# The start of the first FFN: two contraction tiles multiplied before their shift is known

## The chip, the cores and the metric

The kernel runs on one core of one Trainium2 chip. The metric is device time in microseconds (us) of one execution. Five engines work side by side, each on its own list of instructions: TensorE (PE, with its weight loads shown apart as PEld), VectorE (DVE), ScalarE (ACT), GpSimd (POOL) and SyncE (SP), which here issues most transfers. They meet through semaphores.

## The reference, cut to what matters

One layer of a diffusion backbone over 256 latent tokens and 256 context tokens of width 2048. The change touches only the entry of the first half-step FFN:

```
def adaln(x, g, mod, i):
    return rms_norm(x, g) * (1 + mod[:, i + 1, None, :]) + mod[:, i, None, :]

def half_step_ffn(x, mod, i, g, w_up, w_down):
    h = adaln(x, g, mod, i)
    a, b = jnp.split(h @ w_up, 2, axis=-1)
    return x + 0.5 * mod[:, i + 2, None, :] * ((jax.nn.silu(a) * b) @ w_down)
```

`mod` is `silu(c) @ w_mod + b_mod`, with one condition `c` for the latents and one for the context; `i` is 0 here. So the input of the product `h @ w_up` needs two modulation vectors of 2048 numbers for each of the two sequences: the scale `mod[1]` and the shift `mod[0]`. Each is a product of the condition with a 2048 x 2048 slice of `w_mod`, 16 MB to load. The mixer, the second FFN and the final norm follow and are not touched.

## The kernel before

The contraction of 2048 is cut into 16 tiles of 128 rows, k = 0 to 15. All matrix products keep fp32 accuracy by splitting each operand into a rounded high part and a low remainder: `hhi` and `hlo` hold the modulated and transposed tokens, one 512-wide column block per tile (256 context tokens, then 256 latents), and a product is three matmuls, high by high, low weights by high, high weights by low tokens.

The first stage, up to line 700, prepares the modulated tokens tile by tile and at once multiplies them with the first six column blocks of `w_up` (`NPRE = 3` pairs), which collect in six PSUM banks `pre`. It goes through `BLOCKS` (line 47): tile 0 alone, tile 1 alone, then pairs of tiles. For each block it needs the scale and the shift of those tiles and the weights.

- `mod_unit` (line 558) loads 1 MB of modulation weights from `w_m0` into one of four buffers `mraw`, in the order in which `_laid_out` (line 2388) wrote them.
- `mod_sums(i, k0, k1)` (line 565) multiplies such units with the two conditions on TensorE into a bank from `tbank`, of which there are two, and copies the result to a `row` on ScalarE. `i` is 0 for the shift and 1 for the scale.
- `mod_turned` (line 591) transposes the rows on TensorE, and VectorE adds up their four parts and the bias, into `SH` (shift) and `SC` (scale). `scale_of` (line 218) adds one and multiplies by the norm's gain.
- For a pair of tiles, the shift of the first one comes by another way: its weights lie still as rows, and VectorE multiplies them with the spread condition `cB` and sums (line 669). The shift of the second comes by `mod_sums`.
- `x_turned` and `to_hT` transpose the tokens of a tile on TensorE into a bank from `tbank`; `affine_split` (line 382) turns that bank into `hhi` and `hlo`: ScalarE and VectorE both apply scale and shift, and VectorE takes the difference.
- `products` (line 409) is a generator: its first step loads the weights of a block, its second splits them, and each of six further ones multiplies one unit: three matmuls for a block of one tile, six for a pair.

In the loop over `BLOCKS[1:]` (line 657) the products of one block are spread between the sums and transposes of the next one: `steps(prods, n)` puts n units at that place. `AHEAD` says how many units stand before and behind the groups of sums in the first rounds; later it is none before and one behind each group, one behind the row transposes, and what is left (`drain(prods)`) behind the transposes of the tokens. TensorE and VectorE are pinned to the order of the program in this stage, ScalarE until the block of tiles 2 and 3, and SP's loads are pinned too. `idle` issues products with no use, as fillers for waits (`N_IDLE`).

Buffers are taken in turn: whoever takes a third `tbank` waits until all readers of the first one are done, and a load into a fifth `mraw` waits on SP until one of the four before it has been read.

The first tile, in lines 637 to 656, has the shift's unit first, then the scale's, then the weights. When the stage ends, the next column blocks of `w_up` follow on all 16 tiles (`mm3`, line 150), which read the same `hhi` and `hlo`.

Of the kernel before, what the change touches and what calls it, by code (L numbers as in the profile page):

```python
# [19 lines left out]
P = 128  # L20
# [15 lines left out]
AHEAD = {1: (2, 2, 1), 2: (2, 2, 1, 1)}  # L36
# [24 lines left out]
def tile_layer(ctx: ExitStack, tc: tile.TileContext, I: dict, out: bass.AP):  # L61
# [405 lines left out]
    with pool(name="st", bufs=1) as st:  # L467
# [3 lines left out]
        stack = st.tile([32, P], F32, name="stack")  # L471
        pin(nc.vector.tensor_copy(stack[:, :96].rearrange("p (j q) -> p j q", j=3), ident[:32, :32].unsqueeze(1).to_broadcast([32, 3, 32])))
        sel = st.tile([96, P], BF16, name="sel")[:, :32]
# [14 lines left out]
        thirds = st.tile([96, P], BF16, name="thirds")  # L488
        middle = st.tile([96, P], BF16, name="middle")
        over = st.tile([96, P], F32, name="over")  # L490
# [4 lines left out]
        vector[0].tensor_tensor(thirds[64:96], over[64:96], middle[64:96], op=ALU.subtract)  # L495

# [53 lines left out]
        def x_scaled(k, tb):  # L550
            w = lambda x: x[:, k, :].rearrange("p (s c) -> p s c", s=2)
            affine_split(tb.rearrange("p (s c) -> p s c", s=2), 0, ((k, CTX), (k, LAT)), w(hhi), w(hlo))

# [11 lines left out]
        def mod_sums(i, k0, k1, last=iter(())):  # L565
# [17 lines left out]
            row = st.tile([P, 256], F32, tag="row", name="row", bufs=3)[:, :n]  # L583
# [64 lines left out]
        h0 = st.tile([P, 2, 256], F32, tag="h", name="h", bufs=2)  # L648
        hs = [slice(s * 256, (s + 1) * 256) for s in (CTX, LAT)]
        cols = [(SC[:, 0, s, 0:1], SH[:, 0, s, 0:1]) for s in (CTX, LAT)]  # L650
        for s in (CTX, LAT):
            scalar[0].activation(hhi[:, 0, hs[s]], first_tb[:, hs[s]], AF.Identity, scale=cols[s][0], bias=cols[s][1])
        scalar[0].activation(h0[:, CTX], first_tb[:, hs[CTX]], AF.Identity, scale=cols[CTX][0], bias=cols[CTX][1])
        vector[0].tensor_scalar(h0[:, LAT], first_tb[:, hs[LAT]], *cols[LAT], op0=ALU.mult, op1=ALU.add)
        vector[0].tensor_tensor(hlo[:, 0], h0.rearrange("p s c -> p (s c)"), hhi[:, 0].bitcast(F32), op=ALU.subtract)
        others(1, True)
        for k0, k1 in BLOCKS[1:]:
            kk = slice(k0, k1)
            following = products(1, pre, k0, k1, hhi, hlo, middle=True)
            if k1 - k0 == 2:  # L660
                raw = mod_unit()
            ahead = iter(AHEAD.get(k0, ()))
            steps(prods, next(ahead, 0))
            for i in range(2):
                for _ in mod_sums(i, k0 if i else k1 - 1, k1, following if i else iter(())):
                    steps(prods, next(ahead, 3 - (k1 - k0)))
                if not i and k1 - k0 == 2:
# [16 lines left out]
            if k1 - k0 == 1:  # L684
                tb = tbank()
                for s in (CTX, LAT):
                    for t in range(2):
                        x_turned(k0, s, t, tb)
                x_scaled(k0, tb)
            else:  # L690
                for s in (CTX, LAT):
                    drain(to_hT([xs0[s, 0], xs0[s, 1]], 0, s, hhi, hlo, 256 * s, range(k0, k1)))
# [1695 lines left out]
def _laid_out(a):  # L2388
# [23 lines left out]
    def block(k0, k1):  # L2412

        still = [wm[:, 0, k0 * P : (k0 + 1) * P].T[None]] if k1 - k0 == 2 else []
        return still + [units(0, k1 - 1, k1), units(1, k0, k1)]
# [53 lines left out]
```

## Time and profile before

| | |
|---|---|
| median of 3 runs | 2595.6 us (2595.38 to 2599.9) |
| profiled execution | 2594.48 us, span 2592.8 us |
| PE busy | 2566.9 us (99%) |
| DVE busy | 2183.1 us (84%) |
| ACT busy | 1432.8 us (55%) |
| the first stage | up to 133.14 us, when the first product at line 154 starts |
| rounds of a pair of tiles | 13.14 us each from 58.87 us on |

Line 89 in the profile is the helper that pins instructions, so the first stage's instructions show that line; they are told apart by the tiles they write and read: `tr<-mraw,cP` are the modulation sums, `tr<-ident,row` the row transposes, `tr<-ident,xs` the transposes of the tokens, `mm<-hhi,hi`, `mm<-hhi,lo` and `mm<-hlo,hi` the products. A row of the timeline gives the start, the length, the engine, the line, the operation and the count of what was merged; in brackets stands the idle time before it and what ended it. Matmuls overlap their successors, so the step from start to start is the cost of one, not its length.

### The profile page before, as it was taken

The numbers are of one execution on the slowest core, as the hardware profiler recorded it, in microseconds if no ns is written. First come the engines' busy times: TensorE is split into PE (matmuls) and PEld (weight loads), VectorE is DVE, ScalarE is ACT, GpSimd is POOL, SyncE is SP. The second block draws the span as 40 slices with busy tenths as digits, with TensorE's granted clock in tenths as the row PEclk, the third lists the DMA queues.
The fourth block names the chain that finished last, engine by engine and source line by source line (L and its number), as shares of the span: only waits on it lengthen the run. The fifth ranks groups of instructions, "written<-read, shape, count | busy, mean of one in ns | idle before, by whom it ended". The sixth has DMA issues, their size and how long they took to land. (4 is left out here: it accounts for less than half of the span.)

```text
span 2592.8 us, 34296 instructions
## 1 busy us (share of the span) xinstructions
PE 2566.9 (99%) x12716; PEld 2141.8 (83%) x12716; DVE 2183.1 (84%) x2884; ACT 1432.8 (55%) x1838; POOL 221.3 (9%) x273
## 2 busy tenths in 40 slices
PE   8999999999999999999999999999999999999998
PEld 5788888888888888888889989888898888888886
DVE  6788888878888788888887889798889888898987
ACT  4454444545445465444454448456486676667764
POOL 0000000100001100000110000120000000000001
PEclk9999999999999999999999999999999999999999
DMA  9989999999999989889986897776768999999986
GB/s 389 359 215 265 266 288 270 263 275 285 260 292 251 287 248 242 211 223 225 229 258 248 295 327 239 245 278 218 263 239 247 275 275 276 283 287 277 272 251 168
DMA packets 127657, 684.73 MB, mean 264 GB/s; under 512 B 14201, under 2 KB 16761, under 8 KB 64897
## 3 DMA queue, kind: packets, MB, share of 16 engines
q1 hardware_dynamic: 98112, 490.63, 50.6%
q0 software_dynamic: 29376, 191.90, 37.7%
q8 instruction: 100, 1.64, 0.2%
q14 instruction: 69, 0.56, 0.1%
HBM read 664.59 MB, written 17.89 MB: 263 GB/s over the span
## 5 line engine op out<-in xcount | busy, mean ns | idle before, releaser
L130 ACT ACTIVATE hi<-raw 128x1024 fp32r<-128x1024 f32 (+2 forms) x488 | 505.7, 1040 | 411.2 <-PE mm L154 305.5
L131 DVE TENSOR_TENSOR lo<-raw,hi 128x1024 fp32r<-128x1024 f32 (+2 forms) x476 | 569.1, 1204 | 133.3 <-ACT hi L130 112.1
L130 ACT ACTIVATE hi<-chain 128x1024 fp32r<-128x1024 f32 x352 | 372.0, 1060 | 304.6 <-PE mm L154 187.2
L131 DVE TENSOR_TENSOR lo<-chain,hi 128x1024 fp32r<-128x1024 f32 x352 | 426.5, 1221 | 106.3 <-ACT hi L130 99.5
L154 PE MATMUL mm<-hi,hhi 128*128 128x512 f32 (+3 forms) x1024 | 394.0, 385 | 0.0
L154 PE MATMUL mm<-lo,hhi 128*128 128x512 f32 (+3 forms) x1024 | 386.9, 378 | 0.0
L154 PE MATMUL mm<-hi,hlo 128*128 128x512 f32 (+3 forms) x1024 | 386.4, 377 | 0.0
L210 DVE SCALAR_TENSOR_TENSOR junk<-sraw,cBh 128x1024 fp8e5<-128x1024 f32 x192 | 234.4, 1221 | 23.6 <-DMA sraw<-in_w_mt 21.3
L154 PEld LDWEIGHTS mm<-lo,hhi 128*128 128x128 f32 x1024 | 192.5, 188 | 33.9
L154 PEld LDWEIGHTS mm<-hi,hhi 128*128 128x128 f32 x1024 | 192.6, 188 | 31.0
L154 PEld LDWEIGHTS mm<-hi,hlo 128*128 128x128 f32 x1024 | 192.8, 188 | 30.7
L131 DVE TENSOR_TENSOR lo<-ra,hi 128x1024 fp32r<-128x1024 f32 x104 | 126.2, 1221 | 26.4 <-ACT hi L130 22.4
L130 ACT ACTIVATE hi<-ra 128x1024 fp32r<-128x1024 f32 x104 | 110.2, 1062 | 66.5 <-PE mm L154 37.2
L154 PE MATMUL mm<-lo,hid2h 128*128 128x512 f32 (+1 forms) x356 | 137.8, 387 | 0.8 <-DVE lo L131 0.8
L154 PE MATMUL mm<-hi,hid2h 128*128 128x512 f32 (+1 forms) x356 | 137.8, 387 | 0.0
L154 PE MATMUL mm<-hi,hid2l 128*128 128x512 f32 (+1 forms) x356 | 137.7, 387 | 0.0
L154 PE MATMUL mm<-hi,sumshl 128*128 128x512 f32 x400 | 123.2, 389 | 0.0
L740 POOL DMA_DIRECT2D chain<-in_w_up1b x60 | 53.0, 884 | 732.0 <-DVE lo L131 652.9
L210 DVE SCALAR_TENSOR_TENSOR sr<-sr,cBl 128x1024 f32<-128x1024 f32 x84 | 102.1, 1223 | 13.3 <-DMA sr<-in_w_mt 11.9
L154 PE MATMUL mm<-hi,sumshh 128*128 128x512 f32 x352 | 108.4, 389 | 0.0
L154 PE MATMUL mm<-hhi,hi 128*128 128x512 f32 (+1 forms) x288 | 101.3, 352 | 0.0
L154 PE MATMUL mm<-hhi,lo 128*128 128x512 f32 (+1 forms) x288 | 99.0, 344 | 0.0
(505 smaller groups left out, 5449.8 us busy)
## 6 DMA issues: line engine op xcount, KB each, us to landing
raw<-in_w_dn SPq DMA_DIRECT2D x70, 1024.0 KB, 9.1
chain<-in_w_up1b POOLq DMA_DIRECT2D x60, 1024.0 KB, 10.5
sraw<-in_w_mt SPq DMA_DIRECT2D x96, 512.0 KB, 8.2
sr<-in_w_mt SPq DMA_DIRECT2D x81, 512.0 KB, 5.5
raw<-in_w_up1b SPq DMA_DIRECT2D x40, 1024.0 KB, 7.9
mraw<-in_w_m SPq DMA_DIRECT2D x32, 1024.0 KB, 7.5
chain<-in_w_dn POOLq DMA_DIRECT2D x30, 1024.0 KB, 8.3
chain<-in_w_up2b POOLq DMA_DIRECT2D x28, 1024.0 KB, 10.8
```

The costliest lines, as they stand in the source:

```text
L130: scalar[0].activation(hi, src, AF.Copy)
L131: vector[0].tensor_tensor(lo, src, hi.bitcast(F32), op=ALU.subtract)
L154: tensor[0].matmul(out_ap, s, m, start=first and not n, stop=last and n == 2, skip_group_check=skip)
L210: ins = nc.vector.scalar_tensor_tensor(junk() if junk else raw, raw, 1.0, cB[s], op0=ALU.mult, op1=ALU.mult, accum_out=mT[:, i, s, kt, h : ...
L740: accum = lambda dst, src: nc.gpsimd.dma_start(dst, src, accum_op=ALU.add)
```

## The change

For tiles 0 and 1 (`LATER = 2`) the shift is left out at first. Their tokens are multiplied by the scale alone (`scaled`), split and multiplied with the weights as before. The two units of shift weights for these tiles move from the head of the queue to behind the block of tiles 12 and 13 (`SHIFT_AT = 12`), as two units of 256 columns, summed there by `mod_sums(0, 0, LATER)` behind the transposes of the tokens. Then the weights of the two tiles are loaded a second time, 768 KB (`first_weights`). In the last round `shift_products` multiplies them with the two shifts, one column each in a matrix `SHp` of 64 columns, splits the result into high and low parts (`adds`), and `shift_added` adds it to all columns of the six banks with one product each, whose moving operand `owners` picks the rows of a sequence. `shifted` then adds the shift to `hhi` and `hlo` of the two tiles for the later products.

The scale sums of tile 1 move ahead of the first products; tile 1's preparation stands between the products of tile 0. The loop starts at the third block, and `AHEAD` has new entries. The small tiles of the start (`stack`, `sel`, `thirds`, `middle`, `over`) share one buffer with `adds`, and `row` has two buffers in place of three.

```
-AHEAD = {1: (2, 2, 1), 2: (2, 2, 1, 1)}
+AHEAD = {2: (2, 1, 0, 0), 4: (2, 1, 1, 1), 14: (0, 0, 1, 0)}
+LATER, SHIFT_AT = 2, 12
...
+        owner = st.tile([P, 2], F32, name="owner")
+        vector[0].tensor_reduce(owner, ident.rearrange("p (j x) -> p x j", j=4)[:, 0:2], axis=AX.X, op=ALU.add)
+        owners = st.tile([P, 2], F32R, name="owners")
+        vector[0].tensor_copy(owners, owner)
+        SHp = st.tile([P, LATER, 64], F32, name="SHp")
+        nc.gpsimd.memset(SHp, 0.0)
...
-        ready += [mod_unit(), mod_unit()]
+        first_units = [mod_unit()]
         tc.keep_in_program_order(nc.sync.dma_start(vecs, I["vecs"]))
         prods = products(1, pre, 0, 1, hhi, hlo, middle=True)
         steps(prods)
+        first_units.append(mod_unit())
+        following = products(1, pre, 1, 2, hhi, hlo, middle=True)
+        steps(following)
+        first_units += [mod_unit(), mod_unit()]
+        ready += first_units
...
-        drain(mod_sums(0, 0, 1))
+        drain(mod_sums(1, 0, 1))
         first_columns(LAT, 1, r)
-        idle(N_IDLE[4])
         others(2)
-        others(1, True)
-        drain(mod_sums(1, 0, 1))
         mod_turned()
-        idle(N_IDLE[5])
         for s in (CTX, LAT):
             scale_of(0, s, slice(0, 1))
         steps(prods)
+        drain(mod_sums(1, 1, 2))
+        idle(N_IDLE[4])
...
+        def scaled(k, tb):
+            h = st.tile([P, 2, 256], F32, tag="h", name="h", bufs=2)
+            cols = [SC[:, 0, s, k : k + 1] for s in (CTX, LAT)]
+            for s in (CTX, LAT):
+                scalar[0].activation(hhi[:, k, hs[s]], tb[:, hs[s]], AF.Copy, scale=cols[s])
+            scalar[0].activation(h[:, CTX], tb[:, hs[CTX]], AF.Copy, scale=cols[CTX])
+            vector[0].tensor_scalar(h[:, LAT], tb[:, hs[LAT]], cols[LAT], None, op0=ALU.mult)
+            vector[0].tensor_tensor(hlo[:, k], h.rearrange("p s c -> p (s c)"), hhi[:, k].bitcast(F32), op=ALU.subtract)
+
+        def shifted(k):
+            h = st.tile([P, 2, 256], F32, tag="h", name="h", bufs=2)
+            for s in (CTX, LAT):
+                vector[0].scalar_tensor_tensor(h[:, s], hhi[:, k, hs[s]].bitcast(F32), SH[:, 0, s, k : k + 1], hlo[:, k, hs[s]].bitcast(F32), op0=ALU.add, op1=ALU.add)
+            h = h.rearrange("p s c -> p (s c)")
+            scalar[0].activation(hhi[:, k], h, AF.Copy)
+            vector[0].tensor_tensor(hlo[:, k], h, hhi[:, k].bitcast(F32), op=ALU.subtract)
+
+        def first_weights():
+            raw = st.tile([P, 2048], F32, tag="mraw", name="mraw", bufs=4)[:, : LATER * 2 * NPRE * P]
+            src = I["w_pre1"][: LATER * 2 * NPRE * P * P].rearrange("(k p c) -> p k c", k=LATER, p=P)
+            tc.keep_in_program_order(nc.sync.dma_start(raw.rearrange("p (k c) -> p k c", k=LATER), src))
+            again.append(raw.rearrange("p (k c) -> p k c", k=LATER))
+
+        def shift_products():
+            adds.append(st.tile([P, 2 * NPRE * P], F32R, tag="adds", name="adds"))
+            both = SHp.rearrange("p k (j x) -> p k j x", j=2)[:, :, :, 0:2]
+            for j in range(2):
+                vector[0].tensor_copy(both[:, :, j], SH[:, 0, :, 0:LATER].rearrange("p s k -> p k s"))
+            for c in (slice(0, 512), slice(512, 2 * NPRE * P)):
+                b = tbank()[:, : c.stop - c.start]
+                for k in range(LATER):
+                    tensor[0].matmul(b[64 * k : 64 * k + 64], SHp[:, k, :], again[0][:, k, c], start=True, stop=True, tile_position=(0, 64 * k), skip_group_check=True)
+                scalar[0].activation(adds[0][:, c], b, AF.Copy)
+                for o in (32, 96):
+                    q = slice(o, o + 32)
+                    vector[0].tensor_tensor(adds[0][q, c], b[q], adds[0][q, c].bitcast(F32), op=ALU.subtract)
+                yield
+
+        def shift_added():
+            for u in range(2 * NPRE):
+                tensor[0].matmul(pre[u // 2][u % 2], adds[0][:, u * P : (u + 1) * P], owners.unsqueeze(2).to_broadcast([P, 2, 256]), start=False, stop=False, skip_group_check=True)
+
+        scaled(0, first_tb)
+        steps(prods, 2)
+        steps(following)
+        mod_turned()
         for s in (CTX, LAT):
...
+            scale_of(0, s, slice(1, 2))
+        tb = tbank()
+        for s in (CTX, LAT):
+            for t in range(2):
+                x_turned(1, s, t, tb)
+        steps(prods)
+        scaled(1, tb)
         others(1, True)
-        for k0, k1 in BLOCKS[1:]:
+        others(1)
+        drain(prods)
+        prods = following
+        for k0, k1 in BLOCKS[2:]:
...
+            if k0 == SHIFT_AT + 2:
+                mod_turned()
+                steps(prods)
+                for _ in shift_products():
+                    steps(prods)
             steps(prods, next(ahead, 0))
             for i in range(2):
                 for _ in mod_sums(i, k0 if i else k1 - 1, k1, following if i else iter(())):
-                    steps(prods, next(ahead, 3 - (k1 - k0)))
+                    steps(prods, next(ahead, 1))
...
+            for s in (CTX, LAT):
+                drain(to_hT([xs0[s, 0], xs0[s, 1]], 0, s, hhi, hlo, 256 * s, range(k0, k1)))
+            if k0 == SHIFT_AT:
+                drain(mod_sums(0, 0, LATER))
+                first_weights()
+            if k0 > SHIFT_AT:
+                shift_added()
+                for k in range(LATER):
+                    shifted(k)
             drain(prods)
...
+        if k1 <= LATER:
+            return [units(1, k0, k1)]
+        behind = [units(0, 0, LATER)] if k0 == SHIFT_AT else []
+        return [wm[:, 0, k0 * P : (k0 + 1) * P].T[None], units(0, k1 - 1, k1), units(1, k0, k1)] + behind
```

More of the change, by code (lines that the diff above doesn't have):

```diff
@@ L487, in tile_layer @@
         tensor[0].matmul(c3, stack[:, :96], cc, start=True, stop=True)
-        thirds = st.tile([96, P], BF16, name="thirds")
-        middle = st.tile([96, P], BF16, name="middle")
-        over = st.tile([96, P], F32, name="over")
+        thirds, middle = (parts0[:96, c : c + 64].bitcast(BF16) for c in (4 * 64, 5 * 64))
+        over = parts0[:96, P : 2 * P]
         vector[0].tensor_copy(thirds, c3)
@@ L582, in mod_sums @@
                 yield
-            row = st.tile([P, 256], F32, tag="row", name="row", bufs=3)[:, :n]
+            row = st.tile([P, 256], F32, tag="row", name="row", bufs=2)[:, :n]
             scalar[0].activation(row, b, AF.Copy)
@@ L665, in tile_layer @@
                 for _ in mod_sums(i, k0 if i else k1 - 1, k1, following if i else iter(())):
-                    steps(prods, next(ahead, 3 - (k1 - k0)))
-                if not i and k1 - k0 == 2:
+                    steps(prods, next(ahead, 1))
+                if not i:
                     for s in (CTX, LAT):
```

29 lines of the change are left out of this document (5 added, 24 removed).

## The prediction

> **What bounds the kernel now.** I read the busy shares first, then who made TensorE (PE) wait, then the first 133 us stage by stage, since all edits lie there.
>
> ```profile
> span 2592.8 us, 34296 instructions
> PE 2566.9 (99%) x12716; PEld 2141.8 (83%) x12716; DVE 2183.1 (84%) x2884; ACT 1432.8 (55%) x1838; POOL 221.3 (9%) x273
> ```
>
> PE is the bound of the whole. The view of waits of PE from 133 us to the end has seven rows, which sum to 4.3 us; the first and the last:
>
> ```profile
> PE Y L154 <- DVE lo L131: 1.2, 3, 0.6
> ...
> PE mm L154 <- ACT cathi L1808: 0.2, 1, 0.2
> ```
>
> So a microsecond by which the first stage ends earlier or later moves the end by about a microsecond. The first stage in stretches (span, busy time of PE, PEld, DVE, ACT, POOL; clock; DMA share; GB/s):
>
> ```profile
> 10.00:15.00 5.00, 3.58 (x28) 3.04 (x27) 3.98 (x17) 4.54 (x14) 1.18 (x2) 1.00 1.00 421
> ...
> 20.00:40.00 20.00, 16.93 (x163) 11.25 (x167) 10.56 (x25) 7.00 (x14) 0.00 (x0) 0.91 1.00 410
> ...
> 60.00:80.00 20.00, 20.00 (x165) 13.57 (x165) 16.07 (x24) 7.33 (x14) 0.00 (x0) 1.00 1.01 415
> ```
>
> From 20 to 40 us the transfers run full and PE has holes of 3 us, the last long one before 45.39 (below); from 60 us it has none. The change can therefore gain only before 60 us, and whatever PE work or PE wait it puts behind 60 us counts in full. The places of the front (start, length, engine):
>
> ```profile
> 18.44 0.84 PEld L89 LDWEIGHTS tr<-mraw,cP 128*32 128x32 f32 x32 [0.27 <-issue]
> 18.47 1.08 PE L89 MATMUL tr<-mraw,cP 128*32 128x128 f32 x32
> ...
> 19.61 0.28 ACT L89 ACTIVATE row<-tr 128x128 f32<-128x128 f32 x1 [0.15 <-PE tr L89]
> ...
> 20.90 1.02 ACT L89 ACTIVATE hhi<-mm,SH,SC 128x256 fp32r<-128x256 f32 x2 [0.19 <-DVE SC L89]
> ...
> 21.97 0.50 PE L89 MATMUL mm<-hhi,hi 128*128 128x512 f32 x1 [0.82 <-ACT hhi L89]
> ...
> 23.73 0.50 PE L89 MATMUL mm<-hlo,hi 128*128 128x512 f32 x1 [0.57 <-DVE hlo L89]
> ...
> 31.64 0.50 PE L89 MATMUL mm<-hhi,hi 128*128 128x512 f32 x1 [1.12 <-ACT hhi L89]
> ...
> 33.40 0.49 PE L89 MATMUL mm<-hlo,hi 128*128 128x512 f32 x1 [0.56 <-DVE hlo L89]
> ...
> 39.89 1.07 PE L89 MATMUL tr<-mraw,cP 128*32 128x256 f32 x16
> ...
> 42.91 0.23 DVE L89 SCALAR_TENSOR_TENSOR SC<-SC,vecs 128x2 f32<-128x2 f32 x2
> ...
> 44.53 1.03 ACT L89 ACTIVATE hhi<-tr,SH,SC 128x256 fp32r<-128x256 f32 x2
> ...
> 45.39 1.08 PE L89 MATMUL tr<-mraw,cP 128*32 128x128 f32 x32 [1.84 <-DVE h L89]
> 46.41 0.50 PE L89 MATMUL mm<-hhi,hi 128*128 128x512 f32 x1
> 46.63 0.69 DVE L89 TENSOR_TENSOR hlo<-h,hhi 128x512 fp32r<-128x512 f32 x1
> ...
> 50.92 1.07 PE L89 MATMUL tr<-mraw,cP 128*32 128x256 f32 x16 [0.22 <-DMA mraw<-in_w_m]
> ...
> 58.87 1.08 PE L89 MATMUL tr<-mraw,cP 128*32 128x128 f32 x32
> ```
>
> First products: tile 0 at 21.97, tile 1 at 31.64, tiles 2 and 3 at 46.41; at 58.87 the undisturbed rounds begin. One such round, which prices most terms:
>
> ```profile
> 72.02 1.08 PE L89 MATMUL tr<-mraw,cP 128*32 128x128 f32 x32
> ...
> 74.61 1.07 PE L89 MATMUL tr<-mraw,cP 128*32 128x256 f32 x16
> ...
> 79.71 0.49 PE L89 MATMUL tr<-ident,row 128*128 128x128 f32 x3
> 79.95 0.49 PE L89 MATMUL mm<-hhi,hi 128*128 128x512 f32 x1
> ...
> 81.45 1.04 PE L89 MATMUL tr<-ident,xs 128*128 128x128 f32 x8
> 82.24 0.48 PE L89 MATMUL mm<-hhi,hi 128*128 128x512 f32 x1
> ...
> 83.71 0.39 PE L89 MATMUL mm<-hhi,hi 128*128 128x512 f32 x1
> 83.94 0.39 PE L89 MATMUL mm<-hhi,lo 128*128 128x512 f32 x1
> ...
> 85.16 1.08 PE L89 MATMUL tr<-mraw,cP 128*32 128x128 f32 x32
> ```
>
> A 512-wide product takes 0.23 (83.71 to 83.94), a unit of six 1.37, a group of modulation sums with its lead-in 1.23 (2.60 from 72.02 to 74.61, less a unit), three row transposes 0.24, eight transposes of x 0.8, a round 13.14 (72.02 to 85.16).
>
> **The change part by part.** All against the profiled execution: 2594.48 us for a span of 2592.8, 1.1 under the median of 2595.6.
>
> *First product.* The sums for the scale of tile 0 take the place at 16.35 where the shift's stood. Those of tile 1 are pinned on PE ahead of the first product, and their 1 MB now lies behind `vecs` (148 KB) and the first weights (384 KB): 545 KB / 421 GB/s = 1.3 us later. I take that place in the queue as ending at 18.4 now, where the second sums start after 0.27 idle. So: 18.44 + 1.3, sums 1.0, row copy 0.3, `hhi` 1.0: 22.1 against 21.97, **+0.15**. What is saved of row transpose, bias and scale (19.9 to 20.9) is what the later load eats.
>
> *Tile 0 to tile 1.* 9.67 us now. After: 18 products at 0.23 = 4.15, the wait for `hlo` 0.6, transposes 0.24 + 0.4; no load is waited for, because tile 1's scale is summed already. 5.4, so tile 1 starts at 27.5: **-4.1 in all**.
>
> *Tile 1 to tiles 2 and 3.* After: 18 products 4.15, three groups of sums 3.7, row copy 0.4, transposes 1.05: 9.3, to 36.8. The loads allow it, being 2 MB earlier in the queue (5.0 us at 421 GB/s): the last sums of the block, at 39.9 now, come at 32. But scale to both `hhi` takes 2.4 (43.14 to 45.56), and the scale is ready at about 35.4: first product 37.7, against 46.41, with one group of sums still to do that before had done: **lead 8.7 - 1.2 = 7.5**. This also drops the 1.84 wait and most of the slow clock at 34 to 37.
>
> *Tiles 2 and 3 to the round at 58.87.* Before 12.46. After: one more group of sums, +1.2; `hlo` comes 4.2 after the scale (43.14 to 47.32), two units now stand first, +1.3; the wait for a load at 50.92 goes, -0.2 with what stands around it -0.4. And `AHEAD[4] = (2, 1, 1, 1)` uses up all six units before the transposes of x, so nothing covers the wait for a transpose bank: **a stall**, priced below at 1.9. Sum 12.46 + 4.0 = 16.4: round at 54.1, **lead 4.8**. Four loads per round and their buffers stay as they were, so the lead lasts to tile 12.
>
> The stall's rows: PE ends the transposes at 82.24, and the bank is free when VectorE's `h` ends.
>
> ```profile
> 83.60 0.54 DVE L89 TENSOR_SCALAR h<-tr,SC,SH 128x256 f32<-128x256 f32 x1 [2.67 <-ACT h L389]
> ```
>
> 84.14 - 82.24 = 1.9; the row at 45.39 is the same wait, 1.84. Its bounds are 0 (units cover it, as at 72.02) and 2.2 with the sums' lead-in; nearest is 1.84, so 1.9.
>
> *Round of tile 12.* The two deferred groups of sums stand between the transposes of x and the last two units: 2 x 1.23 = 2.5, and their bank has the same wait, 1.9, taken before the units that used to cover it. Behind the waiting sums on PE stand those two units and the whole last round; on SP the two weight buffers that they free. **+4.3**.
>
> *Last round.* Row transposes of the deferred sums 0.2. Two shift products of 64 columns per bank, fp32: sums of 256 columns, four groups side by side, take 1.0 for 16, so 0.25 per 256 columns; 768 columns cost 0.75 if the two groups overlap, 1.5 if not, with lead-in 1.2 to 2.0; I take 1.3, since the sums overlap. Row copy without a unit to cover it 0.4. Adding products: 6 x 0.23 = 1.4. **+3.3**. The reload of 768 KB (1.9 us of transfer) lies behind PE work and the queue's lead; uncovered it costs 1.9. It also holds a weight buffer until the shift products have read it, some 4 us into the round; the last sums' load waits for that buffer on SP, with `ccd` and the next stage's first weights behind it. From issue to landing such loads take, up to 60 us:
>
> ```profile
> DMA to landing us min/median/max: 5.2/9.4/17.5
> ```
>
> The least is that of a short queue, as here; the load is wanted 5 us after its issue: 0.2 late, or 4.4 by the median. I take 0. VectorE gets some 3 us of shifting, and ScalarE two copies; the first weights of the next stage are split long before PE wants them at 133.14:
>
> ```profile
> 120.49 1.23 DVE L131 TENSOR_TENSOR lo<-raw,hi 128x1024 fp32r<-128x1024 f32 x1
> ...
> 133.14 0.39 PE L154 MATMUL mm<-hhi,hi 128*128 128x512 f32 x1
> ```
>
> 11 us of cover; 0, or up to 3 if VectorE's order puts this split behind a late load. Fewer idle fillers and the `owner` preparations lie in waits: 0 (0.4 if not).
>
> Sum: -4.8 + 4.3 + 3.3 = **+2.8**, 2597.3.
>
> *The clock.* One term more. In stretches of 3.41 us:
>
> ```profile
> 20.32:23.73 3.41, 2.03 (x12) 1.32 (x10) 2.72 (x8) 3.22 (x5) 0.00 (x0) 1.00 1.00 418
> ...
> 30.56:33.97 3.41, 1.77 (x11) 1.00 (x15) 1.86 (x3) 1.48 (x3) 0.00 (x0) 1.00 1.01 420
> 33.97:37.38 3.41, 3.41 (x36) 2.73 (x31) 3.38 (x3) 0.28 (x1) 0.00 (x0) 0.50 1.01 375
> ...
> 44.21:47.62 3.41, 2.23 (x37) 1.73 (x38) 3.34 (x6) 2.08 (x5) 0.00 (x0) 1.00 1.00 414
> ```
>
> After a stretch with PE busy 1.77 of 3.41 the clock was 0.50 for the next one; after 2.03 and 2.23 it stayed at 1.00. A stall of 1.9 that falls within one stretch leaves at most 1.5 busy, and the following 3.41 us then do half their work: 1.7 lost. Both new stalls are followed by dense PE work, so nothing absorbs it. Bounds 0 and 3.4 for the two; two times in three each by where the stretches fall. The start adds idle (1.4 before tile 1's sums, 1.0 before the first product) that can cost a third one. I take **+3.4**. The Trainium skill ("TensorE: Matmul & The Clock Gate", section "Why this matters for your kernels") advises against idle gaps over about 3 us, which would leave both stalls at full clock; this trace lost its clock after gaps of 1.12 and 0.56, so the trace decides here. By that rule the sum would be 2597.3.
>
> Total +6.2: 2600.7 on the profiled execution, 2601.8 on the median; **2601.2** between them.
>
> **The rivals.** *No clock loss* (chance 0.23): the stalls straddle stretches or are shorter; 2597.3 to 2598.4. For it: the 1.84 wait at 45.39 cost no clock. Against it: the row at 30.56.
>
> *Everything dear* (0.25): a third slow stretch (1.7), shift products one after the other (0.8), the last load or the split late (1 to 2): 2604 to 2607.
>
> *The lead is kept* (0.10): the two bank waits find cover, say through another order of the instructions, which takes 3.8 off the 2.8: 2593.4. It decides if PE shows no gap behind the transposes of tiles 4 and 5 and of 12 and 13; to pass 2590.4 another 3 us would have to go in the last round. Against it: PE's order is pinned.
>
> **How the numbers follow.** A measurement tells 0.2%, 5.2 us, from no change: slower is above 2600.8, faster under 2590.4. The forecast has 0.42, of which 0.30 lies above 2600.8; with the dear case 0.25, slower is 0.55. Same is 0.12 + 0.23 + 0.05 = 0.40; faster 0.05. The range 2595.0 to 2606.0 leaves out most of the kept lead and the far end of the dear case; the forecast's own is 2599.5 to 2603.5.
>
> **What would show it.** Tile 1's first product near 27.5, tiles 2 and 3 near 37.7; a PE gap of about 1.9 released by `h` near 52 and near 104; clock 0.50 in a stretch behind each; the next stage's first product at 136 without slow stretches, 139 with two. Wrong if the rounds start later than 56 (loads late), if either gap is missing, or if the last round grows by much other than 3.3.

## The result and the profile after

The changed kernel takes 2602.17 us (median of 22 runs), the kernel before 2595.45 us (median of 22 runs beside them). The ratio is 1.0023, with a 95% interval of 1.0016 to 1.003: slower by about 6 us. The profiled execution took 2599.43 us for a span of 2597.7 us, 4.95 above that of before. Helper and product lines have moved by two (L89 is L91, L154 is L156).

Busy time and shares from the page of the changed kernel:

```profile
PE 2569.6 (99%) x12690; PEld 2142.9 (82%) x12690; DVE 2189.3 (84%) x2897; ACT 1431.5 (55%) x1840; POOL 220.0 (8%) x274
```

PE is still the bound of the whole. The timeline of PE in the changed kernel (start, length, operation; in brackets the idle time before it and what ended it):

```profile
20.09 1.52 PE L91 MATMUL tr<-mraw,cP 128*32 128x128 f32 x32 [1.71 <-DMA mraw<-in_w_m]
...
22.84 0.77 PE L91 MATMUL mm<-hhi,hi 128*128 128x512 f32 x1
...
28.19 0.39 PE L91 MATMUL mm<-hhi,hi 128*128 128x512 f32 x1
...
37.81 0.50 PE L91 MATMUL mm<-hhi,hi 128*128 128x512 f32 x1
...
54.22 1.08 PE L91 MATMUL tr<-mraw,cP 128*32 128x128 f32 x32 [1.71 <-DVE h L91]
...
93.75 1.08 PE L91 MATMUL tr<-mraw,cP 128*32 128x128 f32 x32
...
105.92 1.93 PE L91 MATMUL tr<-mraw,cP 128*32 128x256 f32 x32 [1.71 <-DVE h L91]
107.79 0.50 PE L91 MATMUL mm<-hhi,hi 128*128 128x512 f32 x1
...
110.66 0.38 PE L91 MATMUL tr<-ident,row 128*128 128x128 f32 x2
...
112.37 1.08 PE L91 MATMUL tr<-mraw,SHp 128*64 128x512 f32 x4
113.38 0.50 PE L91 MATMUL mm<-hhi,hi 128*128 128x512 f32 x1
...
114.96 0.65 PE L91 MATMUL tr<-mraw,SHp 128*64 128x256 f32 x4
115.55 0.50 PE L91 MATMUL mm<-hhi,hi 128*128 128x512 f32 x1
...
122.60 1.63 PE L91 MATMUL tr<-mraw,cP 128*32 128x256 f32 x16 [1.95 <-DMA mraw<-in_w_m]
124.98 0.66 PE L91 MATMUL tr<-ident,row 128*128 128x128 f32 x2 [0.35 <-DVE SH L91]
...
128.07 1.56 PE L91 MATMUL mm<-owners,adds 128*128 128x512 f32 x6
129.46 0.39 PE L91 MATMUL mm<-hhi,hi 128*128 128x512 f32 x1
...
139.50 0.39 PE L156 MATMUL mm<-hhi,hi 128*128 128x512 f32 x1
```

Read it against the places of before. Tile 0's first product came at 21.97 and now comes at 22.84, tile 1's at 31.64 and now 28.19, that of tiles 2 and 3 at 46.41 and now 37.81. The round that started at 58.87 starts at 54.22: a lead of 4.65. Three rounds later the lead is nearly the same: that round starts at 93.75, and before at 98.31. Then it is spent: the round of tile 12 takes 16.91 (93.75 to 110.66) in place of 13.15, and the last round 28.84 (110.66 to 139.50) in place of 21.68. Before, the last round runs from this row to 133.14:

```profile
111.46 1.08 PE L89 MATMUL tr<-mraw,cP 128*32 128x128 f32 x32
```

The next stage starts at 139.50 in place of 133.14, 6.36 later. From there to the end the two profiles differ by 1.5 the other way (2458.2 against 2459.7).

Of the 7.16 that the last round grew, the rows above show: shift products 1.01 and 0.59, adding products 1.39, the wait for the last load 1.95, the wait for `SH` 0.35, and two more row transposes 0.14. The wait for `hlo` is 0.23 where the kernel before has 0.15, so 0.08 more. That is 5.51. PE's waits from 60 to 138 us in the changed kernel (what waited, on what: us in total, times, longest):

```profile
PE tr L91 <- DMA mraw<-in_w_m: 1.9, 1, 1.9
PE tr L91 <- DVE h L91: 1.7, 1, 1.7
PE tr L91 <- DVE SH L91: 0.4, 1, 0.4
PE mm L91 <- DVE hlo L91: 0.2, 1, 0.2
```

The clock has a part too. Stretches of 3.41 us of the changed kernel (span, busy time of PE, PEld, DVE, ACT, POOL; clock; DMA share; GB/s):

```profile
51.29:54.70 3.41, 1.70 (x30) 1.38 (x31) 1.05 (x2) 2.59 (x6) 0.00 (x0) 1.00 1.00 419
54.70:58.12 3.42, 3.42 (x47) 1.86 (x37) 3.29 (x4) 1.64 (x4) 0.00 (x0) 1.00 1.02 418
102.49:105.90 3.41, 1.72 (x12) 1.30 (x10) 0.73 (x3) 2.09 (x5) 0.00 (x0) 1.00 1.02 398
105.90:109.32 3.42, 3.40 (x39) 2.21 (x40) 1.93 (x3) 1.14 (x3) 0.00 (x0) 1.00 0.80 278
119.55:122.97 3.42, 1.48 (x13) 0.85 (x15) 3.39 (x5) 0.86 (x2) 0.00 (x0) 1.00 1.02 383
122.97:126.39 3.42, 3.07 (x22) 1.65 (x12) 1.48 (x7) 0.38 (x1) 0.00 (x0) 0.50 0.95 386
```

No slow stretch stands behind the wait for a transpose bank that ends at 54.22, nor behind the other at 105.92. One stands behind the wait for the last load, and another, from 20.57 to 23.99, in the front. In the later one PE was busy 3.07 at half speed. An estimate from that is 1.5 of work lost, and 5.51 + 1.5 is 7.0 of the 7.16.

Why the load was late is seen on SP's queue. The row of its issue, and the time from issue to landing of the one transfer in that view of `mraw`:

```profile
115.66 0.34 SPq L567 DMA_DIRECT2D mraw<-in_w_m  x1
```

```profile
DMA to landing us min/median/max: 6.9/6.9/6.9
```

The buffer was held by the weights loaded a second time, until the second shift products had read them at 115.55. The load went out at once after that, landed 6.9 later at 122.6, and PE had wanted it at 120.65.

### The profile page after: what moved, and what is told of

Same layout as the page of the kernel before. It is cut to its first block, busy times and chain, and to the rows that moved or that the text cites. A ratio compares the mean times of both kernels' runs of the same rounds, so it can differ in the third digit from the quotient of the medians.

```text
span 2597.7 us, 34263 instructions
## 1 busy us (share of the span) xinstructions
PE 2569.6 (99%) x12690; PEld 2142.9 (82%) x12690; DVE 2189.3 (84%) x2897; ACT 1431.5 (55%) x1840; POOL 220.0 (8%) x274
## 3 DMA queue, kind: packets, MB, share of 16 engines
q8 instruction: 100, 1.64, 0.2%
## 5 line engine op out<-in xcount | busy, mean ns | idle before, releaser
L156 PE MATMUL mm<-hi,hhi 128*128 128x512 f32 (+3 forms) x1024 | 394.0, 385 | 0.0
L156 PE MATMUL mm<-lo,hhi 128*128 128x512 f32 (+3 forms) x1024 | 386.8, 378 | 0.0
L156 PE MATMUL mm<-hi,hlo 128*128 128x512 f32 (+3 forms) x1024 | 386.5, 377 | 0.0
L156 PEld LDWEIGHTS mm<-lo,hhi 128*128 128x128 f32 x1024 | 192.5, 188 | 33.9
L156 PEld LDWEIGHTS mm<-hi,hhi 128*128 128x128 f32 x1024 | 192.6, 188 | 31.1
L156 PEld LDWEIGHTS mm<-hi,hlo 128*128 128x128 f32 x1024 | 192.8, 188 | 30.6
L156 PE MATMUL mm<-lo,hid2h 128*128 128x512 f32 (+1 forms) x356 | 137.8, 387 | 0.1
L156 PE MATMUL mm<-hi,hid2h 128*128 128x512 f32 (+1 forms) x356 | 137.8, 387 | 0.0
L156 PE MATMUL mm<-hi,hid2l 128*128 128x512 f32 (+1 forms) x356 | 137.7, 387 | 0.0
L156 PE MATMUL mm<-hi,sumshl 128*128 128x512 f32 x400 | 123.1, 389 | 0.0
L156 PE MATMUL mm<-hi,sumshh 128*128 128x512 f32 x352 | 108.3, 389 | 0.0
L156 PE MATMUL mm<-hhi,hi 128*128 128x512 f32 (+1 forms) x288 | 101.4, 352 | 0.0
L156 PE MATMUL mm<-hhi,lo 128*128 128x512 f32 (+1 forms) x288 | 99.0, 344 | 0.0
```

The lines of the kernel that those rows point to most:

```text
L156: tensor[0].matmul(out_ap, s, m, start=first and not n, stop=last and n == 2, skip_group_check=skip)
```

## The experiments

The first reading of the two traces was this theory: the ledger of the prediction holds, the bank waits cost their length and no clock, and what the clock term of 3.4 had stood for was in truth the late last load with its slow stretch. The rivals: that the bank waits are what has to go (the clock theory included), that the wait at 54.22 hides nothing and removing it is worth its length, and that the shift's work is late only for its place. T below is the start of the next stage's first product: 133.14 before, 139.50 in the changed kernel. All edits are to the changed kernel but for the eleventh.

**1. The deferred sums behind the last units.** Does the bank wait near 104 cost the end anything?

```
             if k0 == SHIFT_AT:
+                drain(prods)
                 drain(mod_sums(0, 0, LATER))
```

> The two deferred groups of shift sums stand behind the last two units of products of their round, not ahead of them. Ledger theory (the loss is made of work and waits that can be added up): the wait of 1.7 us for the transpose bank near 104 us goes, since two units of 2.7 us cover it; the round shortens from 16.9 to 15.2 us and the whole by 1.7 us against the changed kernel, to 2600.5; the other two waits stay. Clock theory (most of the loss is slow stretches behind the waits, 1.7 us each): a further 1.1 us on average goes with the slow stretch that this wait can cause, 2599.4. If the wait only moves, nothing is gained and a gap of the same size shows elsewhere in the last two rounds.

2600.09 us against 2596.47, ratio 1.0014 [1.0005, 1.0022]; T 138.40. PE's timeline of it:

```profile
107.12 1.93 PE L91 MATMUL tr<-mraw,cP 128*32 128x256 f32 x32
...
121.30 1.07 PE L91 MATMUL tr<-mraw,cP 128*32 128x256 f32 x16 [1.60 <-DMA mraw<-in_w_m]
```

The sums have no wait now, but 1.1 of the 1.71 is all that T gained: the last load is still 1.60 late with a slow stretch behind it (from 123.29), and PE waits 0.56 for an uncovered row copy. The interval overlaps that of the changed kernel. The late load is a bound of its own.

**2. A buffer of its own for the second load.** The cause of the late load, taken away alone.

```
-            raw = st.tile([P, 2048], F32, tag="mraw", name="mraw", bufs=4)[:, : LATER * 2 * NPRE * P]
+            raw = raw_tile(LATER * 2 * NPRE * P)
```

> The weights that are loaded a second time go to a buffer of the other weights, so the last load of modulation weights no longer waits until the shift products have read theirs. Ledger theory: that load is issued near 108 instead of 115.7 us, lands before it is wanted at 120.7, and the wait of 1.95 us and the late row behind it go: 2 us less than the changed kernel, 2600.2, and with the slow stretch that followed the wait up to 3.2 less. Rival, the transfers themselves bound the last round: the load lands late all the same, since 2.8 MB more stand in the queue, and the wait stays near 2 us.

2601.75 us against 2596.47, ratio 1.0024 [1.0014, 1.0035]; T 138.31. The wait for the load is gone, and another has its place. PE's timeline:

```profile
124.43 0.41 PE L91 MATMUL tr<-ident,row 128*128 128x128 f32 x2 [1.97 <-DVE SH L91]
```

VectorE's timeline of the same kernel, and then that of the kernel before:

```profile
114.67 1.39 DVE L91 TENSOR_TENSOR adds<-tr,adds 32x512 fp32r<-32x512 f32 x2 [2.40 <-ACT adds L696]
...
117.51 2.29 DVE L91 SCALAR_TENSOR_TENSOR junkv<-mraw,cB 128x2048 fp8e5<-128x2048 f32 x1
```

```profile
112.45 2.28 DVE L89 SCALAR_TENSOR_TENSOR junkv<-mraw,cB 128x2048 fp8e5<-128x2048 f32 x1
```

In the last round VectorE sits idle 2.40 for ScalarE's copy of the shift products, takes their remainders, and only then starts the long products for tile 14's shift: at 117.51, where they started at 112.45 before. So VectorE's order was late right behind the load, by nearly the same amount. T gains 1.2, no stretch of the last round being slow here. My theory that the load alone took the clock term's place falls: mending it moves the wait.

**3. The wait at 52 covered.** `AHEAD[4]` leaves units to stand before that bank.

```
-AHEAD = {2: (2, 1, 0, 0), 4: (2, 1, 1, 1), 14: (0, 0, 1, 0)}
+AHEAD = {2: (2, 1, 0, 0), 4: (2, 1, 0, 0), 14: (0, 0, 1, 0)}
```

> The entry of AHEAD for the block of tiles 4 and 5 is (2, 1, 0, 0): two units are kept for behind the transposes of the tokens. Ledger theory: the wait of 1.7 us near 52.5 us goes, the undisturbed rounds start at 52.5 instead of 54.2, 1.7 us less, 2600.5. Rival: the units stood between the sums because the loads of that block land late (the last one near 46 us), so PE waits for loads near 44 to 47 us instead, and nothing is gained.

2603.06 us against 2596.47, ratio 1.0025 [1.0014, 1.0035]. PE's timeline, and then the row of the changed kernel that answers to the last:

```profile
60.01 1.07 PE L91 MATMUL tr<-mraw,cP 128*32 128x256 f32 x16 [1.46 <-DMA mraw<-in_w_m]
...
67.97 1.08 PE L91 MATMUL tr<-mraw,cP 128*32 128x128 f32 x32
```

```profile
67.49 1.08 PE L91 MATMUL tr<-mraw,cP 128*32 128x128 f32 x32
```

The bank wait is gone, and the time is spent in four waits for loads of 2.4 together (0.29, 0.41, 0.27 and the 1.46 shown). The round of tile 8 starts no earlier. So the transfers set the lead, and the stall of `AHEAD[4]` costs nothing that this order could win back.

**4. The lead alone.** No shift for tiles 0 and 1 at all: the calls of the deferred sums, the second load, the shift products, the adding and `shifted` are taken out, and with them the two units of weights and the entry 14 of `AHEAD`. The kernel leaves out the shift of two tiles, so it doesn't compute the whole.

```
-            if k0 == SHIFT_AT + 2:
-                mod_turned()
...
-            if k0 == SHIFT_AT:
-                drain(mod_sums(0, 0, LATER))
-                first_weights()
-            if k0 > SHIFT_AT:
-                shift_added()
...
-        behind = [units(0, 0, LATER)] if k0 == SHIFT_AT else []
+        behind = []
```

> Leaves the shift of tiles 0 and 1 out altogether: no deferred sums, no second load of weights, no shift products, nothing added to the banks or to the tokens. The beginning is that of the changed kernel. Ledger theory: what is left is the lead of the beginning, 4.65 us, so 2590.8, a ratio of 0.998 to the kernel before. Clock theory: the idle stretch at 17 to 22 us and the wait near 52 us each cost a slow stretch more than before, and the gain is at most 2 us. Rival, the lead is lost later: PE's earlier start only meets loads later on, and the ratio is 1.000.

2593.04 us against 2596.47, ratio 0.9991 [0.9982, 1.0000]; T 129.92. The early start alone gives 3.4 us in the medians. One thing differs from all other kernels, in PE's timeline and in the stretches:

```profile
54.20 1.08 PE L91 MATMUL tr<-mraw,cP 128*32 128x128 f32 x32 [1.77 <-DVE h L91]
```

```profile
52.12:55.53 3.41, 1.64 (x36) 1.20 (x35) 1.84 (x4) 2.88 (x7) 0.00 (x0) 1.00 1.02 423
55.53:58.94 3.41, 3.41 (x18) 1.92 (x20) 3.38 (x4) 0.69 (x2) 0.00 (x0) 0.50 0.98 384
```

Here the bank wait is 1.77 long, leaves 1.64 busy, and a slow stretch follows. It costs 1.4: the sums behind the wait start at 54.20, as in the changed kernel (54.22), but the round of tile 8 starts at 68.86 and not at 67.49. So this profile's lead is some 1.4 short of what the start gives without it; whether the other executions have that stretch isn't on record.

**5. The shift's work among the last units.** The sums and the buffer as in 1 and 2, and the shift products, the adding and `shifted` moved into the six units behind the last block. The units of the last round go back between its sums (`AHEAD[14]` is `(0, 1, 1, 1)`), as they stand before the change. Of the edit only the part at the end is shown.

```
+        steps(prods)
+        for _ in shift_products():
+            steps(prods)
+        steps(prods)
+        shift_added()
+        for k in range(LATER):
+            shifted(k)
         drain(prods)
```

> The deferred sums stand behind the last units of their round, the second load of weights goes to a buffer of the other weights, and the shift products, what is added to the banks and the shifting of the tokens move to the six units that end the stage; the last round is then as before the change. Ledger theory: no wait is left behind 60 us; the next stage's first product comes at 133.14 - 4.4 (the lead) + 1.9 (sums) + 0.2 (row transposes) + 2.3 (shift products with lead-in) + 1.4 (adding) = 134.5, so +1.4 against the kernel before, a ratio of 1.0005. If VectorE or a load is late in the last round once more, a wait of 1 us or more shows there and the ratio stays above 1.001. If the clock is the larger part of the loss, no slow stretch is left behind 60 us and the ratio falls to 1.000 or under.

2604.06 us against 2595.98, ratio 1.0028 [1.0019, 1.0038]; T 140.15. PE's timeline:

```profile
115.51 1.07 PE L91 MATMUL tr<-mraw,cP 128*32 128x256 f32 x16 [1.55 <-DMA mraw<-in_w_m]
...
119.66 0.64 PE L91 MATMUL tr<-mraw,cP 128*32 128x256 f32 x8 [1.48 <-DMA mraw<-in_w_m]
```

A miss. PE reaches the last sums before their loads, twice, and `hlo` is 1.02 late. In the changed kernel PE did the shift's work while those loads came; that this is the reason is inferred.

**6. Tile 1's scale weights ahead of tile 0's weights.** The wait of 1.71 at 20.09 and its slow stretch, taken away by an earlier load.

```
+        first_units.append(mod_unit())
         prods = products(1, pre, 0, 1, hhi, hlo, middle=True)
         steps(prods)
-        first_units.append(mod_unit())
```

> The load of tile 1's scale weights stands ahead of tile 0's own weights in the queue, all else as in the changed kernel: it lands 0.9 us earlier, and the idle 1.7 us before its sums shrinks to 0.8. Theory that the transfers set the lead: the products start earlier, but the rounds from 67.5 us on start where they did (67.5 to 68.0), and the time is that of the changed kernel, +6 us on the one before. Rival, the start's idle time counts: 0.9 us less all the way to 139.5, and up to 1 us more if the slow stretch at 21 to 24 us goes.

2603.0 us against 2595.98, ratio 1.0024 [1.0014, 1.0034]. PE's timeline:

```profile
21.78 0.50 PE L91 MATMUL mm<-hhi,hi 128*128 128x512 f32 x1 [0.79 <-ACT hhi L91]
...
60.11 1.07 PE L91 MATMUL tr<-mraw,cP 128*32 128x256 f32 x16 [0.80 <-DMA mraw<-in_w_m]
...
68.04 1.08 PE L91 MATMUL tr<-mraw,cP 128*32 128x128 f32 x32
```

The first product is 1.06 earlier and no stretch at the start is slow, yet the round of tile 8 starts at 68.04 and not at 67.49.

**7. Fillers for the same wait.**

```
+        idle(10)
         drain(mod_sums(1, 1, 2))
```

> Ten products with no use fill the idle time before tile 1's scale sums (1.3 us of work in a gap of 1.7). No slow stretch at 21 to 24 us. Theory that the transfers set the lead: the products start 0.5 us earlier (22.4 instead of 22.8), and the rounds from 67.5 us on start where they did; same time as the changed kernel. Clock theory: without that slow stretch 1 to 1.7 us less, 2600.5 to 2601.

2602.56 us against 2595.98, ratio 1.0022 [1.0011, 1.0032]. With ten filler products in the gap no stretch is slow; the round of tile 8 starts at 67.76. As in 3 and 6, a better start ends in a load wait by 60 us, here of 0.21. In 6 and 7 no stretch of the last round is slow either, and T is 138.96 and 138.02; the medians are no lower for it.

**8. The lead and the deferred sums.** The second load, the shift products, the adding and `shifted` are left out, so this kernel too doesn't compute the whole; the sums and their rows stay.

```
                 drain(mod_sums(0, 0, LATER))
-                first_weights()
-            if k0 > SHIFT_AT:
-                shift_added()
...
-                for _ in shift_products():
-                    steps(prods)
+                steps(prods, 2)
```

> Leaves out the second load of weights, the shift products, what is added to the banks and the shifting of the tokens; the deferred sums stay where the changed kernel has them. Ledger theory: against the kernel without the whole shift (2593.0) it costs two groups of sums and the wait near 104 us, 1.9 + 1.7 + 0.2 of row transposes = 3.8, so 2596.8 or a ratio of 1.0005; and the changed kernel's remaining 5.5 us are the shift's own work (shift products 2.0, adding 1.4), the late last load (2) and the clock. Clock theory: the wait near 104 us brings a slow stretch in two of three runs and the price is 5, 2598.

2597.62 us against 2595.98, ratio 1.0007 [0.9998, 1.0016]; T 135.71. With 4 this makes a ladder, in medians over the kernel before on the same chip: lead alone -3.4, with the deferred sums +1.6, with the shift's work +6.7. The sums with their bank wait cost 5.0 (4.3 and row transposes of 0.2 were predicted) and the shift's work 5.1 (3.1 predicted). The intervals of 4 and 8 reach some 2.3 us to either side. By T the two steps are 5.8 and 3.8, and the first would be larger without the slow stretch in the profile of 4. So the split between the two is known to some 2 us only.

**9 and 10. The shift in the round of tile 8.** Farther from the end, where late loads might be caught up; in 10 with the sums behind the last units too, as in 1. The entry 14 of `AHEAD` moves to 10 with it (not shown).

```
-LATER, SHIFT_AT = 2, 12
+LATER, SHIFT_AT = 2, 8
...
-            if k0 > SHIFT_AT:
+            if k0 == SHIFT_AT + 2:
```

> The deferred sums and the second load stand behind the block of tiles 8 and 9, and the shift products, the adding and the shifting in the round of tiles 10 and 11: two rounds earlier, all else as in the changed kernel. Theory that the last load is late because 2.8 MB more stand ahead of it in the last two rounds and a buffer is held until the shift products have read it: four rounds follow in which the transfers can catch up 1.1 us each (12.0 us of loads in a round of 13.14), so the last load is in time, the wait of 1.95 us and the slow stretch behind it go, and the time is 2 to 3 us under the changed kernel's, +3 to +4.5 on the kernel before. Rival, the stream of loads bounds the whole stage: 0.8 MB more than before end 1.9 us later wherever they stand, the last round waits as long as now, +6.

> As the one before it, and the deferred sums stand behind the last units of products of their round. The wait of 1.7 us for the transpose bank goes too: 1.1 to 1.7 us less than with the sums ahead of the units, +2 to +3 on the kernel before; the work that is added (sums 1.9, shift products 1.8, adding 1.4, row transposes 0.2) less the lead of 4.5 leaves +0.8 as the least. Rival, a bank wait only takes the place of a wait for a load or for VectorE: no difference to the one before it.

2604.73 and 2603.52 us against 2596.8, ratios 1.0034 [1.0021, 1.0046] and 1.0035 [1.0022, 1.0048]; T 140.95 and 142.91. PE's timeline of 9:

```profile
98.12 0.41 PE L91 MATMUL tr<-ident,row 128*128 128x128 f32 x2 [1.96 <-DVE SH L91]
...
115.52 1.09 PE L91 MATMUL tr<-ident,xs 128*128 128x128 f32 x8 [2.50 <-DVE SH L91]
```

The last load is in time, and VectorE is late twice in its place. In 10 a load wait of 2.12 stands at 95.49 and VectorE's at 115.88 is 2.54; three stretches are slow. So this earlier place takes away the late last load and costs as much elsewhere.

**11. Four bank waits in the kernel before.** The disputed price by itself: nothing of the change, only the units of four rounds used up ahead of the transposes of the tokens.

```
-AHEAD = {1: (2, 2, 1), 2: (2, 2, 1, 1)}
+AHEAD = {1: (2, 2, 1), 2: (2, 2, 1, 1)} | {k: (0, 2, 2, 1) for k in (6, 8, 10, 12)}
```

> The kernel before, with one thing changed: in the rounds of tiles 6 to 13 no units of products are left for behind the transposes of the tokens, so the sums that follow wait for the transpose bank, four times 1.7 us. Ledger theory: the time grows by these waits alone, 7 us, a ratio of 1.0027. Clock theory as in the prediction: two of three such waits are followed by a slow stretch that costs 1.7 us more, 11.5 us in all, a ratio of 1.0045, and the granted clock shows two or three slow stretches between 70 and 130 us. If the loads hide part of it, less than 7.

2604.2 us against 2596.8, ratio 1.0031 [1.0019, 1.0043]; T 141.77, +8.6. PE's timeline, its waits from 60 to 142 us, and the stretches around the first:

```profile
74.66 1.08 PE L89 MATMUL tr<-mraw,cP 128*32 128x128 f32 x32 [1.71 <-DVE h L89]
...
119.96 1.08 PE L89 MATMUL tr<-mraw,cP 128*32 128x128 f32 x32 [1.71 <-DVE h L89]
```

```profile
PE tr L89 <- DVE h L89: 6.8, 4, 1.7
```

```profile
72.37:75.78 3.41, 1.70 (x39) 1.26 (x37) 1.58 (x3) 2.84 (x6) 0.00 (x0) 1.00 1.00 419
75.78:79.19 3.41, 3.41 (x20) 2.28 (x24) 3.34 (x5) 1.74 (x3) 0.00 (x0) 1.00 0.71 245
```

Four waits of 1.71, rounds of 15.10 (74.66 to 119.96 is three of them) for 13.14, and full clock behind every one, though the one shown (72.95 to 74.66) lies wholly within a stretch. A bank wait costs 1.96 here, its length with a little lead-in. Four make 7.8 of the 8.6; the rest was there when the rounds began, at 59.74 for 58.87. In the medians the four cost 7.4, where 7 was expected without the clock and 11.5 with it. The ledger's price is confirmed and the clock term isn't.

**12. Both lates mended at once.** The own buffer of 2, and VectorE's long products first in the last round, the shift's work behind the first group of sums. The block at its old place falls out and `AHEAD[14]` becomes `(1, 0, 1, 0)` (not shown).

```
+                if not i and k0 == SHIFT_AT + 2:
+                    mod_turned()
+                    steps(prods)
+                    for c, _ in enumerate(shift_products()):
+                        steps(prods, 1 - c)
```

> As the kernel with the buffer of the other weights for the second load, and in the last round VectorE's two still products (4.6 us) stand ahead of its part of the shift work, which follows the first group of sums instead of opening the round. Theory that VectorE was late there because it stood idle for 3.1 + 2.4 + 0.6 us, waiting in its order for the shift products, before it began the still products: the wait of 1.97 us for VectorE goes, no wait over 0.6 us is left in the last round, the next stage's first product comes near 136 instead of 138.3, and the time is +2.5 to +3.5 on the kernel before. Rival, VectorE has too much work in that round in any order, or a load is late again: a wait of 1.5 us or more stays, and the time with it at +5.5 to +6.5.

2598.17 us against 2598.03, ratio 1.0006 [0.9997, 1.0015]; T 136.74. PE's waits from 60 to 137 us, and the start of VectorE's long products:

```profile
PE tr L91 <- DVE h L91: 1.7, 1, 1.7
PE tr L91 <- ACT row L589: 0.6, 1, 0.6
PE mm L91 <- DVE hlo L91: 0.2, 1, 0.2
```

```profile
109.02 2.29 DVE L91 SCALAR_TENSOR_TENSOR junkv<-mraw,cB 128x2048 fp8e5<-128x2048 f32 x1 [0.97 <-DMA mraw<-in_w_m]
```

VectorE's products start at 109.02 in place of 117.51, no load is late, no stretch of the last round is slow, and in the medians the loss is gone to within what can be measured; the interval lies just apart from that of the changed kernel. T tells a little more: it is 2.76 earlier than in the changed kernel and still 3.60 later than before. The expected +2.5 to +3.5 fits this T and lies at the upper end of the interval, which ends at 3.9 us. So the two lates together were much of the last round's excess. Mending the load alone leaves VectorE late (2); VectorE's order alone was not tried. The kernel doesn't beat the one before, and no run here does with the whole computation. PE work that no order tried here hides is left: deferred sums 1.87 (105.92 to 107.79), shift products 1.6, adding 1.39, row transposes 0.14, 5.0 in all, against a lead of 4.65.

## Why the prediction came true, and where it did not

The total was 6.2 and the medians say 6.7; the sign and the range hold. Step by step, the last two rows being where it failed:

| step | predicted | measured |
|---|---|---|
| first product | 22.1 | 22.84 |
| tile 1 starts | 27.5 | 28.19 |
| tiles 2 and 3, first product | 37.7 | 37.81 |
| undisturbed rounds start | 54.1, lead 4.8 | 54.22, lead 4.65 |
| bank waits near 52 and 104 | 1.9 each | 1.71 each |
| round of tile 12 | +4.3 | +3.76 |
| last round, without clock | +3.3 | +5.5 |
| slow stretches | +3.4, behind the bank waits | 1.5, behind the last load |

*The ledger up to 110 us* held within 0.8 at every place. The first product was 0.7 late because tile 1's load came 1.71 late instead of the 1.4 counted, and the idle there brought a slow stretch. I had named that as possible. It cost the end nothing: 6 and 7 are without it and their rounds start no earlier.

*The stall of `AHEAD[4]`* was sized nearly right and is no cost of that edit. "Four loads per round and their buffers stay as they were, so the lead lasts to tile 12" held: PE's waits show none from 60 us to the one that ends at 105.92. What 3 adds is that transfers set the size of the lead, and PE waits either for the bank or for a load.

*The clock* is the step that failed. It took one row, 1.77 busy with a slow stretch behind it, for a rule: "A stall of 1.9 that falls within one stretch leaves at most 1.5 busy, and the following 3.41 us then do half their work". The waits were 1.71 and left 1.70 and 1.72 of 3.41, which is under 1.77 as well, and the clock stayed at 1.00. So it was the rule that failed, and not only the size by 0.2. The amount was high even by its own terms: "two times in three each" of 1.7 makes 2.3, and the upper bound of 3.4 was entered. Of 23 such waits in the profiles of the changed kernel and the experiments, one was followed by a slow stretch, the one of 1.77 in experiment 4, which left 1.64. The Trainium skill's rule ("TensorE: Matmul & The Clock Gate", section "Why this matters for your kernels": no idle gaps over about 3 us) gave the right outcome for these two waits, and I was wrong to let the row at 30.56 decide against it. As a rule it doesn't hold in these traces, though: the gap of 1.95 before 122.60 is well under 3 us and the next stretch was slow.

*The last round* is where the mis-sized terms sit. The late last load, "0.2 late, or 4.4 by the median. I take 0", measured 1.95: within the bounds given, and the nearer bound was taken because the queue was held to be short there, which no row showed: the landing of 6.9 lies between the 5.2 and the 9.4. Behind it came the slow stretch, 1.5. "VectorE gets some 3 us of shifting" was priced at 0 by the cover of the weights' split. The cover was looked for at the wrong reader: `SH` of tile 14 comes 1.97 late as soon as the load is in time (2). In the changed kernel the late load hides this; the wait for `SH` there is 0.35, and VectorE itself had waited 1.13 for PE's row transpose just before. Shift products and adding products were 1.6 and 1.39 against 1.3 and 1.4, and the row copy of 0.4 was covered.

So the total is right in part by luck. The 3.4 put down to the clock behind the bank waits was not there; 1.95 + 0.35 + 1.5 = 3.8 of the last round was, which the sum had at 0. By the prediction's own sign, "if the last round grows by much other than 3.3", its account of that round is wrong: 5.5 without the clock, 7.16 with it. Of the rivals, "no clock loss" had the mechanism of the bank waits right and its time wrong, "everything dear" named the late load, and "the lead is kept" is refuted by both bank waits. Two of the sums are off by a little that changes nothing: the terms of the first product make 22.04, and those of "the lead is kept" 2593.5.

The rest after T has no edit and still runs from 2458.2 us (the changed kernel, 12) to 2467.6 (11) in the profiles. It goes with PE's waits for VectorE and ScalarE in those later stages: 1.9 us in all in 12, 2.4 in the changed kernel, 4.3 before, 10.2 in 11. Why these waits vary is open. It is a reason to compare T beside the total.

## What to carry to other kernels

Before counting a lead as gain, list the work that was put off as busy time of the bound engine: here 5.0 us of added PE work against 4.65 of lead left nothing to win in any order that was tried. Where a load, an engine's order and the bound engine are all within 2 us of each other, mending one wait may only show the next; take them away together before you judge. A transfer that takes a buffer from a ring delays whoever is a full turn behind it, so price that reader by the measured landing, not at nothing.

## What the runs showed of the hardware that was not expected

In eleven of the profiles (before, after and nine experiments) a slow stretch fixes the phase of the 3.41 us stretches. In these the clock of the next stretch goes with how much PE was busy in one, with the edge near half. From 14 to 139 us, 13 of 13 stretches with 1.64 us or less were followed by clock 0.50, 3 of 14 with 1.68 to 1.80, and none with 1.92 or more. Experiments 6, 7 and 9 have no slow stretch in the first stage. Their phase can be counted back from the turn to half clock near the end (at 2594.27 in 6). Read so, 7 and 9 fit, but 6 doesn't: behind a wait of 2.24, PE was busy 1.56 from 119.60 to 123.01, and the next stretch kept clock 1.00. That makes 13 of 14. Ends of matmuls are modelled, so the hundredths at the edge are not to be trusted, and no run set out to vary the share; it is a pattern in these traces, with experiments 4 and 11 on its two sides and 7, where fillers kept the clock, beside them. The stretches agree in length with the free-running window of 3413 ns in the Trainium skill ("TensorE: Matmul & The Clock Gate", section "What's actually happening"); that page has an idle window bring the slow clock, and here a half idle one was enough.

The row that misled the prediction, 1.77 busy at 30.56 with a slow stretch behind it, is one of the three in the band that goes either way.
